# A transformer block on one core: the mixer's projections reordered, its chains stepped at a finer grain

## The chip, the core and the metric

One core of a Trainium2 chip runs the whole block. The time is device microseconds of one execution; before the change three runs took 1189.47, 1191.2 and 1192.89 us (median 1191.2).

## The reference

The block takes 512 tokens of width 1024 and puts 16 learned tokens beside them (528 in all). Everything is float32.

- `h += 0.5 * swiglu(rms_norm(h))`, hidden width 2816.
- The mixer: `u = rms_norm(h)`, `z = u @ w_in`, split into ten parts. Branch a is a gated linear recurrence in both directions over four heads (`zq_a, zi_a, zf_f, zf_b, zg_a`: query, value, forward and backward gate, output gate). Branch b is softmax attention with eight query heads and two key/value heads (`zq_b, zk_b, zv_b`), normed queries and keys and rotary positions. Then
  `mixed = sigmoid(zgate_a) * (y_a @ w_up_a) + sigmoid(zgate_b) * (y_b @ w_up_b)` and `h += mixed @ w_out`.
- A second half-step swiglu, and the 16 tokens are dropped.

## The kernel before

**Products.** Activations lie feature by token, 128 features a tile. A main product is done in three matmuls per 128 features, on operands parted into a high and a low half (`hi` by a copy on ScalarE, `lo` by a subtraction on VectorE; line 305). Weight tiles arrive by DMA from the SP queue into `raw` and are parted into `whi` and `wlo` (`parts`, line 84), two buffers each, one product ahead. A projection is eight such steps: for 512 tokens one bank of PSUM, for all 528 two. Three banks (`mm`) serve all projections and part of the chains.

**Stages.** First feed-forward to about 376 us of the profile, the mixer to about 840, the second feed-forward to the end. The part that is changed runs from 376 to some 727 us, with the instructions of TensorE, VectorE, ScalarE and GpSimd in an order written by the program itself.

**How that order comes about.** The main line issues the projections of `w_in` one after the other (`zcols`, line 643). Everything that follows from a projection is a *chain*: a generator that issues a few instructions at each step. The class `Order` (line 161) keeps a model of time: `account` adds a duration to each engine (`HOP` is the way from one engine to another, `DRAIN` from a product to its reader), and `pump` (line 230) issues the next step of every chain whose input is ready by that model. `group` (line 299) calls it through `tick` after every 128 features, thus after three products. `need` (line 240) holds the main line until a condition is met, and runs chains meanwhile. All of it happens when the program is built; on the chip each engine works through its list in order and waits by semaphore.

**Chains.** `prepare` (line 836) turns q, k, v into attention operands: for q a square on ScalarE, a small product with ones, a few small operations, the rotation. `scores` (line 862) makes 32 units of 128 queries: product, maximum, exponential; at most two units are out (`out_of`). `turned` (line 894) transposes each unit, parts it, multiplies by the values after four units, and sums the two halves (`ta`, `yb`). `gla` (line 999) builds a head's recurrence in seven levels (copy `ks` on ScalarE, product `gs<-Z,ks`, growth of `Z` and `tot` on VectorE); `gla_finish` (line 1090) ends it. A head's projections are `b` and `f` (gates), `a` (query), `g` (output gate), `i` (value), in `gla_inputs` (line 971); the buffers `Z` and `tot` exist twice, `zi` once, so head 2 waits for head 0 (line 973).

**Order of the projections** (line 625): q0 k0 b0 v f0 a0 g0 i0, q1 b1 f1 a1 g1 i1, s0 q2 b2 f2 a2 g2 i2, s1 q3 b3 f3 a3 g3 i3, then s2 to s6, where s is a gate of branch b (`early`, line 1168). Before q2 and q3 the main line waits for the scores of two heads earlier (line 1190). After s6 it waits for the whole attention, parts the four results, and makes the eight products with `w_up_b` (`branch`, line 1195; lines 1203 to 1224).

Of the kernel before, what the change touches and what calls it, by code (L numbers as in the profile page):

```python
# [6 lines left out]
F32 = mybir.dt.float32  # L7
F32R = mybir.dt.float32r
# [7 lines left out]
P = 128  # L16
# [16 lines left out]
WARM = 12  # L33
LEVELS = (1, 2, 4, 8, 16, 32, 64)
# [119 lines left out]
class Chain:  # L154


    def __init__(self, gen, ready):
        self.gen, self.ready, self.eng, self.wait = gen, ready, None, None


class Order:
# [4 lines left out]
    HOP, DRAIN = 0.12, 0.3  # L166
# [7 lines left out]
    def account(self, eng, op, args, kw):  # L174
# [15 lines left out]
        if eng == "act":  # L190
            d = n * 0.000916 + 0.115
            if "accum_out" in kw:
                d += 0.2
            if not isinstance(kw.get("scale", 1.0), (int, float)):
                d += 0.17
# [18 lines left out]
    def add(self, gen):  # L214
        self.chains.append(Chain(gen, self.cur.ready))
# [14 lines left out]
    def pump(self):  # L230
        while self.chains:
            ch = min(self.chains, key=self.ready)
            if self.ready(ch) > self.t:
                return
            self.step(ch)

    def tick(self, _=None):
        self.pump()
# [54 lines left out]
def block_kernel(tc, xT, wg1, wu1, wd1, w_in, wup, wout, wg2, wu2, wd2, params,  # L293
# [5 lines left out]
    def group(outs, w, xs, tick=None):  # L299
        hi, lo = w  # L300
        n = len(xs)
        for k in range(n):
            sl = slice(k * P, (k + 1) * P)
            xh, xl = xs[k]
            for i, (a, b) in enumerate(((hi, xh), (hi, xl), (lo, xh))):
                for o, cols in outs:
                    pe.matmul(o, a[:, sl], b[:, cols], start=(k == 0 and i == 0),  # L307
                              stop=(k == n - 1 and i == 2))
            if tick:
                tick(0.65 if len(outs) == 1 else 0.68)  # L310

    with (tc.tile_pool(name="persist", bufs=1) as sp, tc.tile_pool(name="wts", bufs=1) as wp,
# [271 lines left out]
        with tc.tile_pool(name="f1", bufs=1) as ft:  # L584
# [40 lines left out]
            order = [Z_QB, Z_KB, Z_FB, Z_VB, Z_FF, Z_QA, Z_G, Z_I]  # L625
            for hd in range(1, HEADS):
                order += [Z_GB + hd - 2] if hd > 1 else []
                order += [c + hd for c in (Z_QB, Z_FB, Z_FF, Z_QA, Z_G, Z_I)]
            plan = [w_in[c] for c in order]
            tiles = [w_in[Z_GB + c] for c in range(KT)] + [wup[c][:, 512:] for c in range(KT)]  # L630
            plan += tiles[HEADS - 2:EARLY] + tiles[KT:KT + 5] + tiles[EARLY:KT] + tiles[KT + 5:]
# [7 lines left out]
        with tc.tile_pool(name="mix", bufs=1) as mp, tc.manual_schedule(engines={pe.engine}):  # L639
# [3 lines left out]
            def zcols(n):  # L643
# [6 lines left out]
                group(outs, w, um, il.tick)  # L650
# [11 lines left out]
            def weights():  # L662
# [4 lines left out]
                w = W.ready.pop(0)  # L667
                if not W.ready:
# [6 lines left out]
                return w  # L675
# [36 lines left out]
            with (tc.tile_pool(name="heads", bufs=1) as hp, tc.tile_pool(name="small", bufs=1) as mn,  # L712
# [3 lines left out]
                oml, noml = lower_bounds()  # L716
                cossin = hp.tile([P, 2, T], F32, name="cossin")
# [93 lines left out]
                def queries_rest(j, z):  # L811
                    act.activation(tq[:, :SEQ], z[:, :SEQ], AF.Square)
                    yield
# [80 lines left out]
                def turned():  # L894

                    for j in range(HEADS):
                        yb.append(mp.tile([P, SEQ], F32, name="yb", tag="yb", bufs=4))
                        for e in range(2):
# [33 lines left out]
                            yield  # L932
                            act.copy(t[d], av[s])
                            yield
                            dve.tensor_tensor(yb[j][d], av[d], t[d], ALU.add)
                            give()
                            yield
                    il.done.add("attention")

# [234 lines left out]
                for gen in (prepare(), scores(), turned(), gla(), gla_finish()):  # L1174
                    il.add(gen)
                queries(0)
                gi = gla_inputs(0)
                kz, ksq = tmp("keys"), hp.tile([P, TP], F32, name="ksq", tag="pr", bufs=3)[:, :T]
                scaled(kz, zcols(T))
                main_input("keys", (kz, ksq))  # L1180
                next(gi)
                vz = tmp("values")
                scaled(vz, zcols(T))
                main_input("values", vz)
                for _ in gi:
                    pass
                for hd in range(1, HEADS):
                    if hd > 1:
                        early(hd - 2)
                        il.need(lambda: f"att{hd - 2}" in il.done)  # L1190
                    queries(hd)
                    for _ in gla_inputs(hd):
                        pass

                def branch(y):
# [140 lines left out]
```

## Time and profile before

| | us |
|---|---|
| median of three runs | 1191.2 |
| profiled execution | 1190.44 |
| its span, first to last instruction | 1188.6 |
| TensorE busy | 1166.7 (98%) |
| VectorE busy | 865.0 (73%) |
| ScalarE busy | 578.5 (49%) |
| GpSimd busy | 98.6 (8%) |
| mean granted TensorE clock | 0.997 |

The span is smaller than the execution's time by what lies before the first and after the last instruction. Matmuls overlap in the records, so a busy TensorE may still hold small losses; a gap is time with no record of it at all. Most mixer instructions carry the line of the wrapper that issues them (289), so they are told apart by the names of their tiles: `mm<-xh,whi` is a main product, `S<-kh,qst` scores, `at<-ident,pr` a transpose, `mm<-ph,vs` values, `mm<-ybh,whi` the product with `w_up_b`.

### The profile page before, as it was taken

To read this page: it belongs to the slowest core of one execution; us is meant where nothing else is said; L and a number is where in the kernel's file an instruction comes from. 1 tells how busy PE (TensorE), PEld (TensorE's weight loads), DVE (VectorE), ACT (ScalarE), POOL (GpSimd) and SP (SyncE) were. 2 spreads that over 40 slices of the span, in tenths; PEclk is the share of its full clock that TensorE was granted. 3 is DMA by queue.
4 is the path that set the end of the run, shared out by engine and by line. 5 is a ranking of instruction groups with operands and counts; after the bars stand their busy time and mean duration, and the time that the engine had idled before them with its cause. 6 is when DMAs were issued, how large, how long until landed. Compare 5 with 4: busy or idle time off the path is not lost.

```text
span 1188.6 us, 19335 instructions
## 1 busy us (share of the span) xinstructions
PE 1166.7 (98%) x7765; PEld 1068.4 (90%) x7765; DVE 865.0 (73%) x1409; ACT 578.5 (49%) x981; POOL 98.6 (8%) x77
## 2 busy tenths in 40 slices
PE   8999999999999999999999989999999999999998
PEld 8999999999999889888888868888879998998997
DVE  7988848847956779797886855454888956966863
ACT  5545525524545366757657553334444634533541
POOL 1001001001103000000000000213001101101100
PEclk9999999999999999999999999999999999999999
DMA  6233322322223221112111012332423233323213
GB/s 235 63 97 133 98 90 89 113 83 107 68 67 116 75 86 57 51 37 71 37 54 53 28 45 98 107 109 95 142 64 132 85 106 110 105 91 109 90 56 123
DMA packets 34233, 106.21 MB, mean 89 GB/s; under 512 B 3936, under 2 KB 4320, under 8 KB 34144
## 3 DMA queue, kind: packets, MB, share of 16 engines
q1 hardware_dynamic: 33984, 104.44, 26.4%
q8 instruction: 61, 1.00, 0.3%
q0 software_dynamic: 160, 0.54, 0.1%
q14 instruction: 28, 0.23, 0.1%
HBM read 102.87 MB, written 2.10 MB: 88 GB/s over the span
## 4 chain that ended last, share of the span: by engine, by line
PE 90%; DVE 5%; ACT 2%; DMA 2%; issue 1%; SPq 0%; POOL 0%; ACTq 0%; DVEq 0%
PE mm L289 21%; PE mm L307 20%; PE mm L484 14%; PE at L484 9%; PE at L307 5%; PE am L307 4%; PE gs L484 4%; PE S L307 4%; PE gs L289 3%; PE am L484 2%; DVE wlo L102 1%; PE S L289 1%; PE at L289 1%; DMA raw<-in_wu 1%; ACT whi L101 1%
## 5 line engine op out<-in xcount | busy, mean ns | idle before, releaser
L101 ACT CAST whi<-raw 128x1024 fp32r<-128x1024 f32 (+2 forms) x179 | 149.9, 839 | 254.2 <-PE mm L307 87.3
L102 DVE TENSOR_TENSOR wlo<-raw,whi 128x1024 fp32r<-128x1024 f32 (+2 forms) x179 | 176.9, 991 | 22.1 <-ACT whi L101 20.0
L289 PE MATMUL mm<-xh,whi 128*128 128x512 f32 (+1 forms) x352 | 115.1, 364 | 1.6 <-DVE tm L289 1.2
L289 PE MATMUL mm<-xh,wlo 128*128 128x512 f32 (+1 forms) x352 | 108.8, 346 | 0.0
L289 PE MATMUL mm<-xl,whi 128*128 128x512 f32 (+1 forms) x352 | 108.6, 346 | 0.0
L102 DVE TENSOR_TENSOR wlo<-sums,whi 128x1024 fp32r<-128x1024 f32 x72 | 87.5, 1217 | 25.3 <-ACT whi L101 25.2
L101 ACT CAST whi<-sums 128x1024 fp32r<-128x1024 f32 x72 | 75.4, 1050 | 62.0 <-DVE sums L128 21.0
L133 POOL TENSOR_TENSOR sums<-raw 128x512 f32<-128x512 f32 x36 | 57.9, 1608 | 495.1 <-DVE wlo L102 485.8
L289 PEld LDWEIGHTS mm<-xh,whi 128*128 128x128 f32 x352 | 62.4, 191 | 9.9 <-DVE tm L289 2.0
L289 PEld LDWEIGHTS mm<-xh,wlo 128*128 128x128 f32 x352 | 62.0, 191 | 8.4
L289 PEld LDWEIGHTS mm<-xl,whi 128*128 128x128 f32 x352 | 62.1, 191 | 4.9
L307 PE MATMUL mm<-hh,wlo 128*128 128x256 f32 (+1 forms) x218 | 63.0, 334 | 0.0
L307 PE MATMUL mm<-hh,whi 128*128 128x256 f32 (+1 forms) x218 | 62.9, 333 | 0.1
L307 PE MATMUL mm<-hl,whi 128*128 128x256 f32 (+1 forms) x218 | 62.9, 332 | 0.0
L484 PE MATMUL mm<-xl,whi 128*128 128x264 f32 (+1 forms) x216 | 61.3, 284 | 0.0
L484 PE MATMUL mm<-xh,whi 128*128 128x264 f32 (+1 forms) x216 | 61.2, 284 | 0.0
L484 PE MATMUL mm<-xh,wlo 128*128 128x264 f32 (+1 forms) x216 | 61.2, 283 | 0.0
L289 ACT CAST whi<-raw 128x1024 fp32r<-128x1024 f32 (+1 forms) x41 | 39.6, 965 | 38.9 <-PE mm L289 32.5
L307 PE MATMUL mm<-xl,whi 128*128 128x512 f32 (+2 forms) x152 | 51.1, 362 | 1.3 <-DVE xl L389 1.3
L307 PE MATMUL mm<-xh,whi 128*128 128x512 f32 (+2 forms) x152 | 50.4, 357 | 1.8 <-ACT xh L388 1.8
L578 DVE SCALAR_TENSOR_TENSOR h<-mm,h 128x512 f32<-128x512 f32 (+2 forms) x40 | 20.9, 544 | 41.4 <-PE mm L307 41.3
L289 DVE TENSOR_TENSOR Z<-Z,tot 128x512 f32<-128x512 f32 (+1 forms) x48 | 40.7, 875 | 13.8 <-PE gs L289 6.8
(354 smaller groups left out, 3593.2 us busy)
## 6 DMA issues: line engine op xcount, KB each, us to landing
raw<-in_wg SPq DMA_DIRECT2D x43, 512.0 KB, 3.6
raw<-in_wu SPq DMA_DIRECT2D x43, 512.0 KB, 3.3
raw<-in_w_in SPq DMA_DIRECT2D x42, 512.0 KB, 3.2
raw<-in_wd SPq DMA_DIRECT2D x48, 384.0 KB, 3.1
raw<-in_wd SPq DMA_DIRECT2D x16, 256.0 KB, 2.6
raw<-in_wup SPq DMA_DIRECT2D x16, 256.0 KB, 2.6
raw<-in_wout SPq DMA_DIRECT2D x8, 512.0 KB, 3.3
h<-in_xT SPq DMA_DIRECT2D x4, 528.0 KB, 5.7
```

The source lines that it names most:

```text
L101: nc.scalar.copy(hi[:, c], src)
L102: nc.vector.tensor_tensor(lo[:, c], src, hi[:, c].bitcast(F32), ALU.subtract)
L133: nc.gpsimd.tensor_tensor(t[:, E], r0[:, E], r1[:, E], ALU.add)
L289: return f(*args, **kw)
L307: pe.matmul(o, a[:, sl], b[:, cols], start=(k == 0 and i == 0), stop=(k == n - 1 and i == 2))
L484: pe.matmul(o, a[:, sl], b[:, kk, :], start=(start and kk == 0 and i == 0), stop=(kk == 3 and i == 2), skip_group_check=True)
L578: dve.scalar_tensor_tensor(h[c][:, cols], o, 0.5, h[c][:, cols], ALU.mult, ALU.add)
```

## The change

- The projections come in the order of the list `MAIN`, with `w` for the values; the generators of the four heads are stepped by it. s0 to s2 are among them (`AMONG` is 3).
- The wait for the scores of two heads earlier moves from the main line into `queries_rest`.
- `group` calls `pump` after every product (or pair of products where there are two banks) instead of after three.
- `pump` gives a chain that is ready a lead; `gla` and `gla_finish` have 5 us, the others none.
- The model's constants change: `HOP` 0.12 to 0.06, `DRAIN` 0.3 to 0.12, two of ScalarE's; VectorE counts as taken until 6.5 at the start.
- `turned` hands the sums `ta` and `yb` to a chain `summed`, which at a head's second half goes on to `parted`: it parts the head's result into `YB`, in the room of earlier tiles.
- The first product with `w_up_b` is made over heads 0 to 2 before the last head's result is needed, and over head 3 afterwards; the next weight tile is then asked for after it (`go_on`, `ahead`).

```
@@ -31,6 +31,11 @@
 EARLY = 7
 EPS = 1e-6
 WARM = 12
+R_READY = 6.5
+LEAD = 5.0
+BEGUN = 1
+MAIN = """q0 k0 b0 f0 a0 w0 g0 i0 b1 f1 q1 a1 g1 i1 q2 s0 q3 s1 b2 f2 a2 g2 i2 b3 f3 a3 g3 i3 s2""".split()
+AMONG = sum(m[0] == "s" for m in MAIN)
 LEVELS = (1, 2, 4, 8, 16, 32, 64)
 FULL = (slice(0, CUT), slice(CUT, T))
 WIDE = slice(512 - CUT, 512 - CUT + T)
@@ -154,8 +159,8 @@
 class Chain:
-    def __init__(self, gen, ready):
-        self.gen, self.ready, self.eng, self.wait = gen, ready, None, None
+    def __init__(self, gen, ready, lead=0.0):
+        self.gen, self.ready, self.eng, self.wait, self.lead = gen, ready, None, None, lead
 class Order:
@@ -163,7 +168,7 @@
-    HOP, DRAIN = 0.12, 0.3
+    HOP, DRAIN = 0.06, 0.12
     def __init__(self):
         self.t, self.free, self.table = 0.0, {}, None
@@ -190,9 +195,9 @@
         if eng == "act":
             d = n * 0.000916 + 0.115
             if "accum_out" in kw:
-                d += 0.2
+                d += 0.25
             if not isinstance(kw.get("scale", 1.0), (int, float)):
-                d += 0.17
+                d += 0.135
             f = args[2] if len(args) > 2 else kw.get("func")
             if f in (AF.Exp, AF.Sigmoid, AF.Sqrt) and f != self.table:
                 self.table = f
@@ -211,8 +216,8 @@
         self.free[eng] = cur.ready = start + d
         cur.eng = eng
-    def add(self, gen):
-        self.chains.append(Chain(gen, self.cur.ready))
+    def add(self, gen, lead=0.0):
+        self.chains.append(Chain(gen, self.cur.ready, lead))
     def ready(self, ch):
         w = True if ch.wait is None else ch.wait()
@@ -229,13 +234,10 @@
     def pump(self):
         while self.chains:
-            ch = min(self.chains, key=self.ready)
+            ch = min(self.chains, key=lambda ch: self.ready(ch) - (ch.lead if self.ready(ch) <= self.t else 0.0))
             if self.ready(ch) > self.t:
                 return
             self.step(ch)
-
-    def tick(self, _=None):
-        self.pump()
     def need(self, cond):
         while not cond():
@@ -296,18 +298,18 @@
     act, dve, pe, pool = (Timed(e, n) for e, n in ((nc.scalar, "act"), (nc.vector, "dve"),
                                                     (nc.tensor, "pe"), (nc.gpsimd, "pool")))
-    def group(outs, w, xs, tick=None):
+    def group(outs, w, xs, tick=None, ks=None):
         hi, lo = w
         n = len(xs)
-        for k in range(n):
+        for k in range(n) if ks is None else ks:
             sl = slice(k * P, (k + 1) * P)
             xh, xl = xs[k]
             for i, (a, b) in enumerate(((hi, xh), (hi, xl), (lo, xh))):
                 for o, cols in outs:
                     pe.matmul(o, a[:, sl], b[:, cols], start=(k == 0 and i == 0),
-                              stop=(k == n - 1 and i == 2))
-            if tick:
-                tick(0.65 if len(outs) == 1 else 0.68)
+                              stop=(k == (HEADS if ks else n) - 1 and i == 2))
+                if tick:
+                    tick()
     with (tc.tile_pool(name="persist", bufs=1) as sp, tc.tile_pool(name="wts", bufs=1) as wp,
           tc.tile_pool(name="psum", bufs=1, space=PSUM) as pp):
@@ -622,13 +624,10 @@
                 if c == KT - 1:
                     rstd([(bank(g)[:, :c.stop - c.start], c) for g, c in zip(("gs", "at"), FULL)], T)
-            order = [Z_QB, Z_KB, Z_FB, Z_VB, Z_FF, Z_QA, Z_G, Z_I]
-            for hd in range(1, HEADS):
-                order += [Z_GB + hd - 2] if hd > 1 else []
-                order += [c + hd for c in (Z_QB, Z_FB, Z_FF, Z_QA, Z_G, Z_I)]
-            plan = [w_in[c] for c in order]
+            first = dict(q=Z_QB, k=Z_KB, w=Z_VB, b=Z_FB, f=Z_FF, a=Z_QA, g=Z_G, i=Z_I, s=Z_GB)
+            plan = [w_in[first[m[0]] + int(m[1])] for m in MAIN]
             tiles = [w_in[Z_GB + c] for c in range(KT)] + [wup[c][:, 512:] for c in range(KT)]
-            plan += tiles[HEADS - 2:EARLY] + tiles[KT:KT + 5] + tiles[EARLY:KT] + tiles[KT + 5:]
+            plan += tiles[AMONG:EARLY] + tiles[KT:KT + 5] + tiles[EARLY:KT] + tiles[KT + 5:]
             for c in range(KT):
                 plan += [w_in[Z_GA + c], wup[c][:, :512]]
             plan += [wout[c] for c in range(KT)]
@@ -647,7 +646,7 @@
                     outs = [(mm()[:, :c.stop - c.start], c) for c in FULL]
                 else:
                     outs = [(mm(), slice(0, SEQ))]
-                group(outs, w, um, il.tick)
+                group(outs, w, um, il.pump)
                 return outs
             def mm():
@@ -659,12 +658,18 @@
                 if state["fifo"]:
                     il.give()
-            def weights():
+            def weights(go_on=True):
                 if not state["fifo"]:
                     return W.next()
                 il.need(lambda: W.ready)
                 w = W.ready.pop(0)
+                if go_on:
+                    ahead()
+                return w
+
+            def ahead():
+
                 if not W.ready:
                     if not W.ahead_raw:
                         W.fetch()
@@ -672,7 +677,6 @@
                     il.add(W.parts(act, dve))
                     il.step(il.chains[-1])
                     W.fetch()
-                return w
             def scaled(dst, outs):
                 for o, cols in outs:
@@ -714,6 +718,7 @@
                 Timed.clock = il
                 state["fifo"] = True
                 oml, noml = lower_bounds()
+                il.free["dve"] = R_READY
                 cossin = hp.tile([P, 2, T], F32, name="cossin")
                 cosS, sinS = cossin[:, 0], cossin[:, 1]
                 nc.gpsimd.dma_start(out=cosS, in_=cosT)
@@ -810,6 +815,8 @@
                 def queries_rest(j, z):
                     act.activation(tq[:, :SEQ], z[:, :SEQ], AF.Square)
+                    if j > 1:
+                        yield lambda: f"att{j - 2}" in il.done
                     yield
                     yield il.has_bank
                     o = mm()
@@ -929,13 +936,39 @@
                             pe.matmul(av, v[:32 + META, 4, :], pmeta, start=False, stop=True)
                             d, s = slice(e * 64, e * 64 + 64), slice(64 - e * 64, 128 - e * 64)
                             t = hp.tile([P, SEQ], F32, name="ta", tag="ta", bufs=1)
-                            yield
-                            act.copy(t[d], av[s])
-                            yield
-                            dve.tensor_tensor(yb[j][d], av[d], t[d], ALU.add)
-                            give()
+                            il.add(summed(j, e, av, t, d, s))
+                            il.chains[-1].eng = "pe"
                             yield
                     il.done.add("attention")
+
+                def summed(j, e, av, t, d, s):
+
+                    yield
+                    act.copy(t[d], av[s])
+                    yield
+                    dve.tensor_tensor(yb[j][d], av[d], t[d], ALU.add)
+                    give()
+                    if e:
+                        yield
+                        yield from parted(j)
+
+                YB = []
+
+                def parted(j):
+
+                    yield lambda: {"att1", f"q{HEADS - 1}", f"att{j}"} <= il.done
+                    if j == 0:
+                        both = [hp.tile([P, TP], F32R, name=n)[:, :SEQ] for n in ("kh0", "kl0")]
+                    elif j == 1:
+                        t = hp.tile([P, 2, T], F32R, name="cossin")
+                        both = [t[:, i, :SEQ] for i in range(2)]
+                    else:
+                        both = [hp.tile([P, SEQ], F32R, name="qst", tag="qst", bufs=4) for _ in range(2)]
+                    act.copy(both[0], yb[j])
+                    yield
+                    dve.tensor_tensor(both[1], yb[j], both[0].bitcast(F32), ALU.subtract)
+                    YB.append(both)
+                    il.done.add(f"y{j}")
                 def main_input(name, arg):
                     inputs[name] = arg, il.main.ready
@@ -1171,51 +1204,49 @@
                     gate(sg)
                     sgs.append(sg)
-                for gen in (prepare(), scores(), turned(), gla(), gla_finish()):
-                    il.add(gen)
-                queries(0)
-                gi = gla_inputs(0)
-                kz, ksq = tmp("keys"), hp.tile([P, TP], F32, name="ksq", tag="pr", bufs=3)[:, :T]
-                scaled(kz, zcols(T))
-                main_input("keys", (kz, ksq))
-                next(gi)
-                vz = tmp("values")
-                scaled(vz, zcols(T))
-                main_input("values", vz)
-                for _ in gi:
-                    pass
-                for hd in range(1, HEADS):
-                    if hd > 1:
-                        early(hd - 2)
-                        il.need(lambda: f"att{hd - 2}" in il.done)
-                    queries(hd)
-                    for _ in gla_inputs(hd):
-                        pass
-
-                def branch(y):
-                    w = weights()
-                    b = mm()
-                    group([(b, slice(0, SEQ))], w, y, il.tick)
-                    return b
-
-                for c in range(HEADS - 2, EARLY):
+                for gen, lead in ((prepare(), 0.0), (scores(), 0.0), (turned(), 0.0), (gla(), LEAD), (gla_finish(), LEAD)):
+                    il.add(gen, lead)
+                def keys():
+                    kz, ksq = tmp("keys"), hp.tile([P, TP], F32, name="ksq", tag="pr", bufs=3)[:, :T]
+                    scaled(kz, zcols(T))
+                    main_input("keys", (kz, ksq))
+
+                def values():
+                    vz = tmp("values")
+                    scaled(vz, zcols(T))
+                    main_input("values", vz)
+
+                gi = [gla_inputs(hd) for hd in range(HEADS)]
+                for m in MAIN:
+                    what, j = m[0], int(m[1])
+                    if what in "qs":
+                        (queries if what == "q" else early)(j)
+                    elif what in "kw":
+                        (keys if what == "k" else values)()
+                    else:
+                        next(gi[j], None)
+
+                def branch(js, w=None, b=None, go_on=True):
+
+                    if w is None:
+                        w, b = weights(go_on), mm()
+                    group([(b, slice(0, SEQ))], w, YB, il.pump, js)
+                    return (w, b) if js[-1] < HEADS - 1 else b
+
+                for c in range(AMONG, EARLY):
                     early(c)
-                il.need(lambda: "attention" in il.done)
-                YB = []
-                ybh = hp.tile([P, 4, SEQ], F32R, name="ybh", tag="ph")
-                ybl = hp.tile([P, 4, SEQ], F32R, name="ybl", tag="pl")
-                ready = il.t
-                for j, y in enumerate(yb):
-                    il.main.ready = ready
-                    split((ybh[:, j, :], ybl[:, j, :]), y, slice(0, SEQ))
-                    YB.append((ybh[:, j, :], ybl[:, j, :]))
+                il.need(lambda: f"y{HEADS - 2}" in il.done)
+                begun = [branch(range(HEADS - 1), go_on=c + 1 < BEGUN) for c in range(BEGUN)]
+                il.need(lambda: f"y{HEADS - 1}" in il.done)
                 mixb = []
                 for c in range(KT):
                     if c == 5:
                         sgs.append(tmp()[:, :SEQ])
                         gate(sgs[-1])
-                    b = branch(YB)
+                    b = branch(range(HEADS - 1, HEADS), *begun[c]) if c < BEGUN else branch(range(HEADS))
+                    if c == 0:
+                        ahead()
                     act.activation(sgs[c], sgs[c], AF.Sigmoid)
                     m = sgs[c] if c < 4 else mp.tile([P, SEQ], F32, name="mixb", tag="yb", bufs=4)
                     dve.tensor_tensor(m, b, sgs[c], ALU.mult)
```

## Rows read from the trace of the kernel before

**Rows 1.** Page, part 1: busy us, share of the span, instructions.

```profile
...
PE 1166.7 (98%) x7765; PEld 1068.4 (90%) x7765; DVE 865.0 (73%) x1409; ACT 578.5 (49%) x981; POOL 98.6 (8%) x77
...
```

**Rows 2.** Windows, whole mixer: start:end, length, busy us of each engine, clock, DMA.

```profile
...
376.50:732.00 355.50, 344.52 (x2081) 299.17 (x2080) 274.95 (x532) 204.11 (x390) 2.80 (x13) 0.99 0.17 59
...
```

**Rows 3.** Windows, the mixer's stretches with the larger gaps.

```profile
...
386.20:393.30 7.10, 5.64 (x34) 5.64 (x34) 4.67 (x18) 1.01 (x2) 0.00 (x0) 0.76 0.23 76
501.00:514.00 13.00, 11.60 (x78) 9.68 (x76) 8.33 (x22) 6.44 (x21) 0.00 (x0) 1.00 0.00 1
602.00:608.20 6.20, 4.79 (x25) 4.10 (x24) 5.21 (x10) 2.36 (x5) 0.00 (x0) 0.72 0.23 85
...
684.00:706.00 22.00, 18.67 (x97) 13.93 (x95) 11.16 (x27) 11.55 (x28) 0.00 (x0) 1.00 0.07 25
706.00:732.00 26.00, 25.25 (x112) 20.52 (x112) 14.12 (x22) 10.69 (x21) 0.00 (x0) 1.00 0.33 112
...
```

**Rows 4.** Timeline, start of the mixer: start us, length, engine, operation.

```profile
...
383.12 0.41 PE L289 MATMUL mm<-xh,whi 128*128 128x256 f32 x2
...
385.80 0.41 PE L289 MATMUL mm<-xh,wlo 128*128 128x256 f32 x2
...
386.23 0.68 DVE L289 TENSOR_TENSOR tm<-mm,R 128x512 f32<-128x512 f32 x1
...
386.95 0.63 ACT L289 ACTIVATE tq<-tm 128x512 f32<-128x512 f32 x1 [2.43 <-DVE tm L289]
...
387.68 1.02 PE L289 MATMUL mm<-kones,tq 128*128 128x2 f32 x8 [1.46 <-issue]
...
```

**Rows 5.** Timeline of PE, before head 2's projections.

```profile
...
511.17 0.87 PE L289 MATMUL mm<-ident,on 128*128 128x128 f32 x4 [0.60 <-ACT on L289]
...
513.14 0.48 PE L289 MATMUL mm<-xh,whi 128*128 128x512 f32 x1
...
```

**Rows 6.** Timeline, around the wait at 602.

```profile
...
601.73 0.58 ACT L289 COPY ta<-mm 64x512 f32<-64x512 f32 x1 [2.33 <-PE mm L289]
...
603.36 0.61 ACT L289 COPY ks<-Z 128x512 f32<-128x512 f32 x1
...
604.03 1.52 PE L289 MATMUL gs<-Z,ks 128*128 128x128 f32 x8 [1.41 <-ACT ks L289]
...
```

**Rows 7.** Timeline, from the last transposes to the second `up` product.

```profile
...
684.00 0.60 PE L289 MATMUL at<-ident,pr 128*128 128x128 f32 x4
...
689.29 0.58 ACT L289 COPY ta<-mm 64x512 f32<-64x512 f32 x1 [2.79 <-PE mm L289]
...
691.79 0.50 PE L289 MATMUL mm<-ybh,whi 128*128 128x512 f32 x1 [1.04 <-ACT ybh L289]
...
693.84 1.28 ACT L289 ACT_TABLE_LOAD   x1
...
695.13 0.63 ACT L289 ACTIVATE mixb<-mixb 128x512 f32<-128x512 f32 x1
...
695.80 0.69 DVE L289 TENSOR_TENSOR mixb<-mm,mixb 128x512 f32<-128x512 f32 x1 [1.15 <-ACT mixb L289]
696.40 1.28 DVE L289 TENSOR_TENSOR wlo<-raw,whi 128x512 fp32r<-128x512 f32 x2
...
697.14 0.50 PE L289 MATMUL mm<-ybh,wlo 128*128 128x512 f32 x1 [1.32 <-DVE wlo L289]
...
```

**Rows 8.** Timeline, first score unit and first recurrence product.

```profile
...
434.25 0.40 PE L289 MATMUL S<-kl,qst 128*128 128x256 f32 x2
...
434.68 0.71 DVE L289 TENSOR_REDUCE nm<-S 128x1 f32<-128x528 f32 x1 [1.03 <-PE S L289]
...
436.79 0.48 PE L289 MATMUL mm<-xh,whi 128*128 128x512 f32 x1
...
437.11 0.39 PE L289 MATMUL mm<-xl,whi 128*128 128x512 f32 x1
...
437.34 0.39 PE L289 MATMUL mm<-xh,wlo 128*128 128x512 f32 x1
...
```

## The prediction

> **What bounds the kernel now.** First the page's busy times: TensorE is busy for 98% of the span [rows 1], so the time is the length of TensorE's queue plus its gaps. Then the same view cut to the mixer: of 355.50 us TensorE is busy 344.52, so 10.98 us are gaps, while VectorE (274.95) and ScalarE (204.11) have room [rows 2]. The diff touches only the mixer. Then the mixer cut into stretches, until each larger gap stood alone [rows 3]; the gap of a stretch is its length less its PE column:
>
> - 386.2 to 393.3: 7.10 − 5.64 = 1.46 us, and the granted clock is 0.76, so 7.1 × 0.24 = 1.70 us more go to the slow level (1.2 GHz);
> - 501 to 514: 1.40 us;
> - 602 to 608.2: 6.20 − 4.79 = 1.41 us, and at clock 0.72 another 6.2 × 0.28 = 1.74 us;
> - 684 to 706: 3.33 us, and 706 to 732: 0.75 us;
> - all the rest together: 10.98 − 8.35 = 2.63 us.
>
> That is all there is to win: 10.98 + 1.70 + 1.74 = 14.4 us, 1.2% of the run. The timeline was read last, around each gap, to see who ended it.
>
> **The change part by part.** Every product, eviction and transfer of before is still issued, in another order, so its busy time cancels. The order on SP's weight queue changes with the plan; each weight tile still goes through the same two buffers one product ahead, and POOL gets nothing new. What counts is what each gap becomes.
>
> *Start (R_READY, finer steps).* TensorE ran k0's products until 386.2, then stood until the square of q0 was there: 24 matmuls in pairs from 383.12 to 385.80, so 12 pairs, eviction at 386.23, square at 386.95, the small product at 387.68 [rows 4]. By the planner's new arithmetic q0 ends at 24 × 0.2266 = 5.44; VectorE is held until 6.5, the eviction takes it to 7.20, the square to 7.84; a pair of k0 counts 0.247, so the small product goes in behind pair 10 (5.44 + 2.47 = 7.91). That is two pairs earlier than before, while nothing on VectorE ahead of the eviction changes. TensorE waits for the same moment with 0.5 us less work done: cost +0.5 us, and the clock drop stays. Bounds: −1.5 (the gap goes) to +1.0 (two more pairs).
>
> *Order of the projections.* At 501 to 514 the main line stands at head 2's `b`, which may not start until head 0's recurrence is done (it needs that head's `Z` buffer); TensorE has only chains left, waits 0.60 for `on`, and main products come back at 513.14 [rows 5]. In the new order `b2` is the 19th projection and not the 17th, so two projections of at least 5.4 us each lie ahead of it and cover 1.40 us. The wait for the scores of head 0, formerly in the main line ahead of q2, moves into a chain. Gain 1.4; at worst 0. If the cover failed it would cost the 1.4 again.
>
> *Sums apart.* At 602 the chain's product waits 1.41 us for `ks`; on ScalarE `ks` (603.36) stands behind the copy `ta` (601.73), which had to wait for the attention product, and a weight conversion [rows 6]. With the sums in a chain of their own the next transposes no longer wait behind `ta`, but `ta` still takes its place on ScalarE and holds its bank. Gain between 0 and 1.41 + 1.74 = 3.15; I take 2.0, nearer the top because the shorter planned eviction brings the bank back sooner in the plan.
>
> *Steps between any two products, priority for the recurrence, new constants.* Before, a chain was asked after three products (0.68 us), now after one (0.23 to 0.25), so a TensorE step waits about 0.22 us less. The planned way from a product to its reader falls from 0.42 to 0.18 us; in the trace two products of a score unit begin at 434.25, last 0.25 by the planner, and the reduction starts at 434.68, so the truth is 0.18 [rows 8]. A score unit has two such hops: 32 × 2 × (0.22 + 0.24) = 29 us of latency, and with two units in flight some 15 us of the 250 us from the first scores to the last transposes (434.25 to 684.00) [rows 7, 8]. The same steps cost TensorE: the first main product after a chain product in plain f32 takes 0.32 us (436.79 to 437.11), the next 0.23 (437.11 to 437.34) [rows 8]. By the code there are 104 such chain steps; I count 83 returns to main products in the timeline, so splitting the shared ones costs at most 21 × 0.09 = 1.9 us. I take +1.0 (bounds 0 and 1.9).
>
> *Results split at once, first `up` product begun with three heads.* Before, the last transposes came at 684.00, the last sum began at 689.29, the first product on the result at 691.79, and a weight part held the second group until 697.14 [rows 7]. If the attention ends 7.8 us earlier against the main products (684.00 to 691.79), all but the last of these gaps go; the 15 us above, and q3 being asked for six projections sooner, say it does. What is late next is the weight of the second `up` product: its parts are now asked for only after the first product is complete, so on VectorE its `wlo` stands behind `mixb`, which waits for the product: 0.18 to the reader, 0.69 for `mixb` and 1.28 / 2 = 0.64 for `wlo`, less two products of 0.23 already possible: 1.1 us [rows 7, 8]; if ScalarE starts its work only then, the table load 1.28 and the sigmoid 0.63 come on top, 3.0 us [rows 7]. I take 1.2 left of 3.33 + 0.75: gain 2.9 (bounds 0 and 4.1). The load of 1.28 us is seen to be all there is: the sigmoid starts at its end [rows 7]. The Trainium skill (ScalarE: Activation LUTs, "What ACT_TABLE_LOAD costs") adds a drain of 1.38 us to such a load, some 2.66 us for a switch; by that the worse case would be 4.3 us and its gain nil; the trace does not agree.
>
> *Rest.* Of 2.63 us of small waits I take 0.9 away, and put 0.5 on for new ones (bounds −2.6 and +3).
>
> Sum: +0.5 − 1.4 − 2.0 + 1.0 − 2.9 − 0.9 + 0.5 = −5.2 us. The profiled execution took 1190.44 (span 1188.6 and 1.84 around it), which makes 1185.2; the median of the runs shown is 0.8 above it, so 1191.2 − 5.2 = **1186.0 us**.
>
> **Rivals.** *Nearly all gaps go* (1180): everything but the start, 14.4 − 1.46 − 1.70 = 11.3 us. For it: the gaps are few and each has a cause that the change touches. Against: three of the terms are only half touched, and the finer steps cost up to 1.9.
>
> *One wait for another* (1191): the new order is another single draw of such collisions. For it: the start stall stays, and the small ones of 2.63 us occur without any cause that is removed. Then only the order's 1.4 us is kept, and the start takes 0.5 and the returns 1.0: 1191.2 + 0.1.
>
> *Steps too early, slower* (1197): the old plan gave each TensorE step 0.24 us of reserve above the measured 0.18, and some 0.34 by the coarse asking; the new one gives none and 0.12. There are some 144 TensorE steps in chains (104, 32 scores, 8 attention products). If each then holds the queue for 0.08 us on average, 11.5 us come in place of the 0.5 for new waits: 1186.0 + 11.0 = 1197. It decides from (5.2 + 0.5) / 144 = 0.04 us per step, where the forecast's gain is gone. For it: [rows 6] show a main queue held by one early step for 1.41 us. Against: what the planner leaves out on TensorE (the 0.09 of a return, for one) makes its products later than planned. The Trainium skill (TensorE: Matmul & The Clock Gate, "Step-by-step") says that only weight loads are pulled ahead and matmuls stay in program order. The trace agrees: main products stood behind `gs` those 1.41 us. In the same case lies an attention that ends after the main products because the recurrence goes first.
>
> *The change does not act*: finer steps give the same order in effect; within 0.3% like the second rival.
>
> **How the numbers follow.** Forecast 0.50, nearly all gaps 0.13, one wait for another (with no effect) 0.25, slower 0.12. About 0.3%, 3.6 us, is what a measurement of this kernel can tell from no change. The forecast's own range is 1182 to 1189, of which about a tenth of all the chance is inside 0.3% of 1191.2. A part of the second rival falls below that bound too. So faster 0.62, same 0.26, slower 0.12. The range 1179.5 to 1192.5 runs from nearly all gaps to the second rival.
>
> **What would show it.** Right: no main-less stretch before `b2`; the gap near 602 and its clock drop gone, one drop left, at the start; the `up` products follow the last early product with at most about 1.2 us, on `wlo`; gaps in the mixer 5 to 7 us. The small product for q0 waits about 2 us. Wrong: many new short waits of PE on ACT `ks` or `ph` (steps too early); a wait on `yb` parts (attention late); a mixer that is as long with fewer gaps (the returns cost more than 1.9).

## The result and the profile after

The changed kernel takes 1183.16 us (median of four runs, 1182.73 to 1185.06) against 1190.74 beside it: 0.9938 of before, 95% interval 0.9919 to 0.9956, so some 7.4 us faster. The forecast was 1186.0 us, a gain of 5.2; the measured time lies inside its range of 1182 to 1189. The profiled execution is the slowest of the four (1185.06); its clock also dropped once in the first feed-forward (0.57 on average from 87 to 91 us), which the change doesn't touch.

The first lines of the page after, span and busy times, are to be read against [rows 1]; TensorE does the same 7765 matmuls:

```profile
span 1183.2 us, 19343 instructions
...
PE 1166.2 (99%) x7765; PEld 1070.7 (90%) x7765; DVE 864.4 (73%) x1409; ACT 579.0 (49%) x981; POOL 99.0 (8%) x77
...
```

These are the mixer's stretches (start:end, length, then busy us of PE, PEld, DVE, ACT, POOL, then clock, DMA share and GB/s); they are to be read against [rows 2, 3]. The mixer's first product comes 2.5 us later than before, so places are shifted by that:

```profile
...
379.00:727.00 348.00, 341.47 (x2080) 298.93 (x2079) 274.12 (x532) 204.03 (x390) 3.11 (x13) 0.99 0.17 60
387.00:396.00 9.00, 7.05 (x46) 6.87 (x46) 6.79 (x23) 0.63 (x1) 0.00 (x0) 0.81 0.22 75
396.00:568.00 172.00, 172.00 (x1088) 152.59 (x1086) 142.25 (x279) 101.85 (x191) 0.44 (x4) 1.00 0.18 62
568.00:577.00 9.00, 7.21 (x39) 6.35 (x39) 8.45 (x20) 8.04 (x14) 0.00 (x0) 0.81 0.17 60
577.00:684.00 107.00, 106.93 (x676) 93.79 (x676) 88.50 (x162) 68.91 (x134) 0.52 (x2) 1.00 0.12 43
684.00:692.50 8.50, 6.54 (x35) 4.70 (x34) 4.29 (x8) 5.49 (x11) 0.00 (x0) 1.00 0.00 0
692.50:704.00 11.50, 11.24 (x63) 9.78 (x64) 4.75 (x17) 3.77 (x14) 0.00 (x0) 1.00 0.27 93
704.00:727.00 23.00, 22.50 (x100) 18.16 (x100) 12.84 (x20) 9.65 (x19) 0.00 (x0) 1.00 0.30 104
...
```

Gaps are length less PE: 348.00 − 341.47 = 6.53 us where there were 10.98. The wait at the start is 1.95 us, longer than before. From 396 to 568 there is none, so the stretch at 501 to 514 is gone, and so are the small waits at the ends of projections. The gap at 602 is gone and a new one stands at 568 to 577, 1.79 us, with a clock drop as before (0.81, so 1.7 us). The end has 1.96 + 0.26 + 0.50 = 2.72 us.

The next view says who ended TensorE's waits (engine, tile, releaser: us in total, times, longest; "issue" means that the profile shows no releaser, and this one is the wait of q0's small product at 390.14):

```profile
...
PE mm L291 <- DVE wlo L291: 2.7, 2, 2.2
PE mm L291 <- issue: 1.9, 1, 1.9
PE mm L291 <- DVE zi L291: 1.5, 1, 1.5
...
```

The view of gaps shows too little. The record of a 512-column product lasts 0.39 us and the next product starts 0.23 us after it does [rows 8], so the first 0.16 us of a wait are hidden under the record before. So the waits were also counted from start to start, from the first main product of the mixer to the first of the next stage, `mm<-yah`. From each interval the median interval of that product before the change is taken off; what is left is a long wait where it is over 0.2 us. What the clock drops cost lies mostly in the last row:

| | before | after |
|---|---|---|
| length of this part, us | 355.25 | 347.93 |
| the 2078 products at their median intervals | 332.11 | 332.11 |
| long waits | 15.14 | 8.36 |
| first products after plain f32 ones (times) | 5.70 (84) | 6.57 (89) |
| all smaller differences | 2.31 | 0.89 |

So 7.32 us are won in this part, and most of it is long waits (6.8).

### The profile page after: what moved, and what is told of

Same layout as the page of the kernel before. It is cut to its first block, busy times and chain, and to the rows that moved or that the text cites. A ratio compares the mean times of both kernels' runs of the same rounds, so it can differ in the third digit from the quotient of the medians.

```text
span 1183.2 us, 19343 instructions
## 1 busy us (share of the span) xinstructions
PE 1166.2 (99%) x7765; PEld 1070.7 (90%) x7765; DVE 864.4 (73%) x1409; ACT 579.0 (49%) x981; POOL 99.0 (8%) x77
## 4 chain that ended last, share of the span: by engine, by line
PE 92%; DVE 3%; ACT 2%; DMA 2%; issue 1%; SPq 0%; POOL 0%; ACTq 0%; DVEq 0%
PE mm L291 21%; PE mm L309 21%; PE mm L486 15%; PE at L486 9%; PE at L309 5%; PE am L309 5%; PE gs L486 4%; PE S L309 4%; PE gs L291 3%; PE am L486 2%; PE S L291 1%; DVE wlo L107 1%; PE at L291 1%; DMA raw<-in_wu 1%; ACT whi L106 1%
## 5 line engine op out<-in xcount | busy, mean ns | idle before, releaser
L291 PE MATMUL mm<-xh,whi 128*128 128x512 f32 (+1 forms) x352 | 111.7, 354 | 1.8 <-DVE zi L291 1.5
L291 PE MATMUL mm<-xl,whi 128*128 128x512 f32 (+1 forms) x352 | 111.4, 354 | 0.0
L309 PE MATMUL mm<-xh,wlo 128*128 128x512 f32 (+2 forms) x152 | 50.2, 356 | 0.0
```

Of the source, the lines that this page charges most:

```text
L291: return f(*args, **kw)
```

## Experiments

Each kernel was timed beside the kernel before, and the ratio is to that. "Waits" are the long waits counted as above, "part" is the length of this part of the mixer; both are of the one profiled execution, with its clock drops, and that can lie some us off the median (1194.37 for e12, 1187.36 for e7).

| kernel | median us | ratio, 95% interval | waits us | part us |
|---|---|---|---|---|
| changed | 1183.16 | 0.9938 (0.9919 to 0.9956) | 8.36 | 347.93 |
| e1 VectorE taken until 8.7 | 1180.59 | 0.9919 (0.9906 to 0.9931) | 6.58 | 344.91 |
| e2 weight asked earlier | 1179.87 | 0.9918 (0.9905 to 0.9931) | 5.37 | 346.16 |
| e3 order of before | 1185.72 | 0.9966 (0.9954 to 0.9978) | 9.34 | 349.87 |
| e4 results parted at the end | 1187.22 | 0.9971 (0.9959 to 0.9983) | 9.48 | 351.03 |
| e5 both, e1 and e2 | 1175.92 | 0.9876 (0.9863 to 0.9889) | 3.59 | 340.06 |
| e6 coarse steps | 1192.16 | 1.0009 (1.0000 to 1.0017) | 14.71 | 355.74 |
| e7 `HOP`, `DRAIN` of before | 1189.44 | 0.9993 (0.9982 to 1.0003) | 14.65 | 352.45 |
| e8 sums in the old chain | 1191.53 | 1.0005 (0.9995 to 1.0015) | 14.71 | 354.53 |
| e9 drain 0.10 | 1183.95 | 0.9936 (0.9924 to 0.9948) | 8.62 | 348.22 |
| e10 drain 0.15 | 1184.63 | 0.9951 (0.9937 to 0.9965) | 8.41 | 347.91 |
| e11 no lead | 1194.13 | 1.0029 (1.0016 to 1.0042) | 15.90 | 358.91 |
| e12 finer steps alone, on before | 1189.19 | 0.9985 (0.9972 to 0.9998) | 14.56 | 357.36 |

**e1.** One constant is changed: `-R_READY = 6.5` `+R_READY = 8.7`

> The changed kernel with VectorE counted as taken until 8.7 us instead of 6.5 at the start of the plan. Theory (the start wait is a plan that asks too early): the small product for q0 goes some nine pairs of k0 later, its 2.1 us wait goes, and with it the clock drop behind it (1.7 us): 1183.2 - 3.8 = 1179.4. Rival (TensorE has to wait for R in any case, since q0 and k0 hold all three banks): the wait moves to b0's first product, 1183 within 1 us.

The theory holds. These are the windows of the start (386 to 395) and of the later wait (columns as above):

```profile
...
386.00:395.00 9.00, 9.00 (x62) 8.32 (x61) 7.79 (x26) 1.69 (x2) 0.00 (x0) 1.00 0.21 71
564.00:573.00 9.00, 7.20 (x41) 6.53 (x41) 8.39 (x20) 8.26 (x15) 0.00 (x0) 0.81 0.20 60
...
```

Of 1.95 us gap and 0.81 clock at the start nothing is left; the small product for q0 goes in at 389.05, 0.18 us after its square is done. One new wait of 0.55 us at the end of a projection (403.5) took a part of it back (1180.6, not 1179.4).

**e2.** The second product's parts are asked for with the first product:

```
-                begun = [branch(range(HEADS - 1), go_on=c + 1 < BEGUN) for c in range(BEGUN)]
+                begun = [branch(range(HEADS - 1)) for c in range(BEGUN)]
...
-                    if c == 0:
-                        ahead()
```

> The changed kernel with the second up product's weight parts asked for when the first one begins, not after it. Theory (its wlo stands behind the first mixb on VectorE): the 2.3 us wait on wlo in the second up product goes, 1183.2 - 2.3 = 1181. Rival (ScalarE and VectorE are the bound there: the table load, two sigmoids and the parts have to be done anyway): the wait moves to a bank or to the third product, 1183 within 1 us.

The theory holds, and the wait of 0.67 us in the fifth `up` product went too. In the timeline of e2 `wlo` (687.52) now stands ahead of `mixb` (691.20) on VectorE, and the second product's third matmul (689.13) waits for nothing:

```profile
...
687.52 0.69 DVE L291 TENSOR_TENSOR wlo<-raw,whi 128x512 fp32r<-128x512 f32 x1
...
689.13 0.39 PE L291 MATMUL mm<-kh,wlo 128*128 128x512 f32 x1
...
691.20 0.69 DVE L291 TENSOR_TENSOR mixb<-mm,mixb 128x512 f32<-128x512 f32 x1 [3.00 <-ACT mixb L291]
...
```

**e3.** `MAIN` is q0 k0 b0 w0 f0 a0 g0 i0 q1 b1 f1 a1 g1 i1 s0 q2 b2 f2 a2 g2 i2 s1 q3 b3 f3 a3 g3 i3; the rest is as changed.

> The changed kernel with the projections in the order of before (s0 and s1 among them), everything else of the change kept. Theory (two more projections ahead of head 2's first one cover the wait for head 0's recurrence): a stretch without main products before b2 is back, with 1.4 to 2.6 us of waits, 1183.2 + 2 = 1185. Rival (the finer steps and truer constants make the recurrence end early enough in any order): 1183 within 1 us and no such stretch.

The size came (though the two intervals just overlap), the place did not. There is no stretch without main products before `b2`; more than half of the waits are at the end, mostly on the last head's result (`qst`, `yb`):

```profile
...
PE mm L291 <- DVE qst L291: 1.8, 1, 1.8
PE mm L291 <- DVE wlo L291: 1.0, 1, 1.0
PE mm L291 <- ACT qst L291: 0.6, 1, 0.6
PE mm L291 <- DVE yb L291: 0.5, 1, 0.5
...
```

The last level of the recurrence (`gs<-Z,ks`) is at 692 there, at 679 in the changed kernel, and its growth of `Z` stands on VectorE ahead of the parting of the last result. The wait ahead of i2 that the changed kernel has at 569 to 572 (2.3 us from start to start) is not there.

**e4.** The results are parted after the whole attention (`split` into `ybh`, `ybl`, as before), all eight products go over four heads, and there is no `begun`.

> The changed kernel with the four results parted together after the whole attention, and no up product begun with three heads. Theory (parting at once takes the end of the attention off TensorE's path): the waits from the last transposes to the second up product go from 3.3 us back towards the 5.7 of before, 1183.2 + 2.4 = 1185.6. Rival (the attention merely ends earlier, the parting costs only its own 0.6 to 1.3 us): 1184.

It is slower (0.9971 to 0.9938). Among TensorE's waits in e4 are these:

```profile
...
PE mm L291 <- ACT on L291: 2.2, 1, 2.2
...
PE mm L291 <- DVE wlo L291: 1.5, 2, 1.0
...
```

The parting itself costs 0.4 us, `wlo` less than in the changed kernel, and a wait of 2.2 us on `on` at 661 is new. So the tail looks no worse. But e4 differs in one thing more: without `go_on` it asks for the second product's parts with the first, as e2 does, and e2 has none of these waits on `wlo` and 0.3 us in the tail, where e4 has 2.3 (both from start to start). Beside e2, parting at once and beginning with three heads are worth some 2 us in the tail. What the rival says also holds: the attention ends early without them, its last transposes at 672.8.

**e5.** This is e1 and e2 together.

> The changed kernel with both mends: VectorE counted as taken until 8.7 us, and the second up product's weight parts asked for when the first begins. Theory (the two waits are apart, 300 us from each other, so the gains add): the changed kernel's 0.9938 of before goes by 0.0019 and 0.0020 to 0.990, some 1178. Rival (a later start shifts the plan, and other collisions take one of the gains): 0.992, 1180.5.

The waits add exactly: 4.77 us less than in the changed kernel, where e1 took 1.78 and e2 2.99. The time, 1175.92, is the fastest of all, 15 us below the kernel before, and its ratio falls by more than the two together (0.0062 for 0.0019 + 0.0020), though not clear of their intervals. In the profile the clock never drops in the mixer, where the changed kernel has two drops of 1.7 us each. Why it stays up is not shown.

**e6.** `tick()` comes after the three products, as before; all else is as changed.

> The changed kernel with chains asked only after three products, as before. Theory (the finer steps shorten every hop through TensorE and so end the attention and the recurrence earlier): waits near the end of the mixer grow, returns to main products fall by some 5 (0.5 us), together 1185 to 1187. Rival (the order and the constants do the work, the step does not): 1183 within 1 us.

All of the gain is gone, more than the theory said. The returns to main products fell from 89 to 79, where it said some 5, but the waits are 14.71. The longest stands in the second `up` product. In its timeline the table load, the first `mixb`, and twelve small operations of the recurrence's end (697.09 to 699.26) come before `wlo` on VectorE:

```profile
...
694.52 1.28 ACT L291 ACT_TABLE_LOAD   x1
...
696.48 0.69 DVE L291 TENSOR_TENSOR mixb<-mm,mixb 128x512 f32<-128x512 f32 x1 [5.31 <-ACT mixb L291]
...
697.09 0.16 DVE L291 TENSOR_SCALAR xo<-ss 128x4 f32<-128x4 f32 x1
...
699.26 0.16 DVE L291 SCALAR_TENSOR_TENSOR yo<-ao,yo 128x4 f32<-128x4 f32 x1
699.34 1.29 DVE L291 TENSOR_TENSOR wlo<-raw,whi 128x512 fp32r<-128x512 f32 x2
...
700.08 0.80 PE L291 MATMUL mm<-kh,wlo 128*128 128x512 f32 x1 [4.79 <-DVE wlo L291]
...
```

**e7.** The two ways of the model are set back, ScalarE's constants are not: `-HOP, DRAIN = 0.06, 0.12` `+HOP, DRAIN = 0.12, 0.3`

> The changed kernel with the model's ways of before, 0.12 and 0.3 us. Theory (a plan that takes products and evictions for slower than they are holds the main line for banks that are free, and puts chain products ahead of it): waits of 0.5 us at the ends of projections are back, 1185 to 1186. Rival (the longer way is a reserve that spares TensorE waits on late inputs): fewer waits than 8.4 us in the mixer, 1181.

It is more than the theory said again. The waits of some 0.55 us at the ends of projections are back (before the products at 404.6, 428.9 and 641.6), as expected, but the longest is another: at 582.11 TensorE waits 4.60 us for `pl`, which stands on VectorE behind twelve small operations, a step of the recurrence and the partings of two results:

```profile
...
577.21 0.17 DVE L291 TENSOR_SCALAR xo<-ss 128x4 f32<-128x4 f32 x1
...
580.07 0.68 DVE L291 TENSOR_TENSOR kl<-yb,kh 128x512 fp32r<-128x512 f32 x1
580.67 0.69 DVE L291 TENSOR_TENSOR cossin<-yb,cossin 128x512 fp32r<-128x512 f32 x1
581.27 0.68 DVE L291 TENSOR_TENSOR pl<-at,ph 128x512 fp32r<-128x512 f32 x1
...
582.11 1.08 PE L291 MATMUL at<-ident,pr 128*128 128x128 f32 x4 [4.60 <-DVE pl L291]
...
```

**e8.** `ta` and `yb` stand in `turned` again, and `il.add(parted(j))` follows them.

> The changed kernel with the attention's sums back in the chain that transposes, the parting of results still in a chain of its own. Theory (the sums' 1.5 us stand in the way of the next transposes once per four units, eight times): the attention ends up to 12 us later and the last of it shows at the end of the mixer, 1184 to 1186. Rival (two units in flight hide it): 1183 within 1 us.

The time is above the theory's figures: waits 14.71, spread over some fifteen places, 8.1 of it after 680. The last transposes are at 681.6 (676.2 in the changed kernel, with its mixer starting some 2 us later), so the attention does end about 8 us later, in line with the bound of 12.

**e9, e10.** `DRAIN` is 0.10 and 0.15 instead of 0.12.

> The changed kernel with the planned drain 0.10 us instead of 0.12, which says almost nothing new about the chip. Theory (the gain is in the plan's structure): within 2 us of 1183.2, waits in the mixer's queue 7 to 10 us. Rival (the changed kernel is a lucky draw of collisions, and any small shift draws again): waits anywhere from 7 to 15 us, and a time up to 1190.

> The changed kernel with the planned drain 0.15 us instead of 0.12. Theory (structure): within 2 us of 1183.2, waits 7 to 10 us. Rival (a lucky draw): waits anywhere from 7 to 15 us, a time up to 1190, and no relation to what the drain 0.10 gives.

The theory's figures came: in both the same waits stand at the same places, 2.1 for q0, 1.7 and 0.6 at the later bank wait, 2.3 in the second `up` product. But the two runs hardly test the rival, since they hardly re-order anything: with TensorE's order laid beside that of the changed kernel by tile names, some 60 and 40 of the part's 2078 products stand elsewhere. The runs that move many (e3, e4, e6, e7, e8, e11: some 400 to 1100) are all slower, by 0.3 to 0.9%, and four of them are about as slow as before. So these shifts of `DRAIN` don't undo the gain, but that the changed plan is a lucky, or well chosen, draw among larger re-orderings is not excluded.

**e11.** `-LEAD = 5.0` `+LEAD = 0.0`

> The changed kernel without the recurrence's lead of 5 us. Theory (with a question after each product few chains are ready at the same time, so the lead hardly decides): a plan that differs little, within 2 us of 1183.2. Rival (the lead carries the recurrence through and so keeps the end of the mixer free): recurrence products late in the up products, 1186 to 1190.

The theory fell. Without the lead the last transposes come at 656.5, some 18 us earlier against the start of the mixer, and the last level of the recurrence at 687.7, some 10 us later. The main line, which needs the recurrence's buffers, stalls in between: no main product runs from 567.2 to 587.3, ahead of b3. Among TensorE's waits are these:

```profile
...
PE mm L291 <- DVE wlo L291: 2.7, 2, 2.2
PE S L291 <- ACT pr L291: 2.0, 2, 1.4
PE mm L291 <- DVE yb L291: 2.0, 1, 2.0
...
PE mm L291 <- ACT on L291: 1.9, 2, 1.5
...
```

**e12.** This is the kernel before with `tick()` after each product and nothing else.

> The kernel before with one part of the change alone: chains asked after every product. Theory (the parts act only together; finer steps in the old order with the old ways move the collisions and leave the end of the attention at the end of the mixer): within 2 us of 1190.7. Rival (the finer step is what brings the gain, since taking it out took all of it): 1184 to 1186.

It is nearer to the theory: 0.9985. The stretch before `b2` is still there (no main product from 500.4 to 520.0), with waits of 0.84, 0.61 and 2.43 us that end at 511.8, 513.5 and 517.3.

Three parts were not taken away alone: the moved wait for the scores of two heads earlier, ScalarE's two constants, and VectorE's start at 6.5.

## Why the prediction was right, step by step

It was right in direction and in what bounds the kernel, the waits in TensorE's queue, and its gain was short by about 2.2 us (the ratio's interval is 5.2 to 9.6 us; in the profiled part it is 7.3). That it came so near is partly luck. From start to start, the terms were worth: start +0.5, order −2.5, sums apart +0.9, returns +0.9, results split −2.4, the rest (small waits) −3.2, all smaller differences −1.4. The sums missed by 2.9 us; order and rest, which won 1.1 and 2.8 more than forecast, and the smaller differences, which had no price, made up for it. Of its own signs, the stretch before `b2` is gone, gaps are 6.5 us and q0 waits 2 us, as said; but there are two clock drops and not one, and the second `up` product waits 2.3 us on `wlo` and not 1.2.

- *Start, +0.5*: this is right to the tenth by gaps, 1.46 to 1.95 us, with the drop kept and the small product behind ten pairs of k0, as worked out. e1 shows the cause: the plan asks too early.
- *Order, −1.4*: the stretch is gone. But e3 has the old order and no such stretch, and e12 has it: in the changed kernel either the order or the other parts do away with it. That the two projections cover it is therefore not shown. e6, the new order with coarse steps, has no such stretch before `b2` either, but one of 10.8 us ahead of q3 (495.9 to 506.7) with a wait of 2.2 us in it. What the order is worth (0.9966 against 0.9938) is a balance: less waiting at the end of the mixer, against the wait at 569 that e3 does not have.
- *Sums apart, −2.0 at 602*: this term failed. The wait at 602 went, but one of the same size with the same drop came at 569: 1.41 + 1.74 became 1.79 + 1.71. In the timeline after, g2's eviction `zi` (570.41) stands on VectorE behind the small operations and two others, `nm` and `qst`, and i2's two banks come free with it and with the attention's sum `yb`:

```profile
...
566.69 0.17 DVE L291 TENSOR_SCALAR xo<-ss 128x4 f32<-128x4 f32 x1 [1.89 <-ACT on L291]
...
568.88 0.16 DVE L291 SCALAR_TENSOR_TENSOR yo<-ao,yo 128x4 f32<-128x4 f32 x1
...
569.22 0.48 PE L291 MATMUL mm<-xh,wlo 128*128 128x512 f32 x1
...
569.69 0.69 DVE L291 TENSOR_TENSOR qst<-tm,qst 64x512 fp32r<-64x512 f32 x1
...
570.41 0.69 DVE L291 TENSOR_TENSOR zi<-mm,R 128x512 f32<-128x512 f32 x1
...
571.13 0.69 DVE L291 TENSOR_TENSOR yb<-mm,ta 64x512 f32<-64x512 f32 x1
...
571.16 0.39 PE L291 MATMUL mm<-xh,whi 128*128 128x256 f32 x1 [1.45 <-DVE zi L291]
...
```

That the three banks are the scarce thing here was read from the order of these rows; no run took it away. e8 shows that the sums apart matter, and there most of the waits lie at the end, not at 602.
- *Finer steps, lead, constants*: the cost was right (returns 84 to 89, +0.9 for +1.0). The lead was given no term, and without it the whole gain is gone (e11). The attention does end earlier: its last transposes come 297.1 us after the mixer's first product, 307.4 before the change. These 10.3 us are more than the 7.8 that were needed and less than the 15 worked out. But the shorter planned way, which was given half of them, is not what brings them: with the old way (e7) they come after 284.4 us, with coarse steps (e6) after 305.8.
- *Results split, −2.9*: measured −1.4 by gaps (3.33 + 0.75 to 2.72), −2.4 by starts. The mechanism named as next was the right one, with a wrong size: I took 1.2 for the wait on the second product's `wlo`, and it is 2.3, since ScalarE's table load came only after the first product had begun, near the upper bound of 3.0. These are the rows after, to be read against [rows 7]:

```profile
...
684.74 0.39 PE L291 MATMUL mm<-kh,whi 128*128 128x512 f32 x1
...
689.46 1.28 ACT L291 ACT_TABLE_LOAD   x1
...
690.75 0.63 ACT L291 ACTIVATE mixb<-mixb 128x512 f32<-128x512 f32 x1
...
691.42 0.69 DVE L291 TENSOR_TENSOR mixb<-mm,mixb 128x512 f32<-128x512 f32 x1 [4.11 <-ACT mixb L291]
...
692.02 1.28 DVE L291 TENSOR_TENSOR wlo<-raw,whi 128x512 fp32r<-128x512 f32 x2
...
692.76 0.50 PE L291 MATMUL mm<-kh,wlo 128*128 128x512 f32 x1 [2.16 <-DVE wlo L291]
...
```

The sigmoid again starts when the load of 1.28 us ends. e2 shows that the place in VectorE's queue was the cause.
- *Rest, −0.9 and +0.5*: this term was mis-sized; 2.63 us became 0.07. Together with the part of each wait that gaps don't show, that is more than the missing 2.2 us; it makes up for the sums as well.

Of the rivals, "nearly all gaps go" and "steps too early" are contradicted by the changed kernel's waits: 8.36 us are left, at nine places, and only four of these are as short as 0.2 to 0.3 us. "One wait for another" did not come as priced, for the waits nearly halved; but 569 is one such place, and as an account of why this plan is faster than its neighbours it stands open (e9, e10).

What the terms could not show is that they don't add. The finer steps, the shorter ways, the sums apart and the lead each cost about the whole gain when taken away alone (e6, e7, e8, e11), and the first of them alone on the old kernel is worth 0.15%. Each of these plans has its long waits at other places. Why just these plans collide was seen in single places (e6, e7), not settled as a rule.

## What to carry to other kernels

When an order is planned from a model of time, look first where the model starts from a wrong state (here a busy VectorE) and where a request is put behind work that has to wait for its result: both were a line or two here, and each was worth about a third of the whole change (by the ratios 2.3 and 2.4 of 7.4 us). Count waits by start-to-start intervals, not by gaps in the busy time. Don't price the parts of a re-plan one by one: test the whole, its neighbours, and each part taken away, and see by how much each run re-orders the plan before calling it a test.

## What was not expected of the chip

The same wait costs different clock. The start wait of 1.95 us is followed by a mean clock of 0.81 over the nine us in the changed kernel and of 0.66 in e2, whose rows there are the same:

```profile
...
386.00:395.00 9.00, 7.05 (x37) 6.86 (x36) 6.60 (x23) 0.63 (x1) 0.00 (x0) 0.66 0.20 70
568.00:577.00 9.00, 7.20 (x37) 6.18 (x37) 8.33 (x21) 7.82 (x15) 0.00 (x0) 0.81 0.18 60
...
```

The wait of 1.8 us near 569 was followed by a drop in both, and by none in e5, where it stands at 565 to 567:

```profile
...
386.00:395.00 9.00, 9.00 (x61) 8.28 (x60) 7.79 (x26) 1.68 (x2) 0.00 (x0) 1.00 0.19 60
563.00:572.00 9.00, 7.20 (x49) 5.97 (x48) 8.29 (x22) 7.82 (x15) 0.00 (x0) 1.00 0.18 60
...
```

So the drop to 1.2 GHz behind a wait of this size cost nothing, 1.7 us (9 × 0.19) or, in e2, 3.1 us within these nine (9 × 0.34) and 3.4 in all, since the low level lasted from 388.9 to 395.8. Nor does the longest wait decide it: the 2.2 us at 692.76 in the changed kernel were followed by no drop (clock 1.00 from 692.50 to 704).

The first main product after a plain f32 product took some 0.08 us longer in every kernel (0.32 for 0.23 us at 512 columns), in all 5.7 us before and 6.6 after, and no longer after scores.
